# Closing LayerNorm of a two-layer trunk: a gate folded into the last weights, a square root by Sqrt and one Newton step, and two column parts centred on ScalarE and GpSimd

## Chip, cores and metric

One core of one Trainium2 chip runs the whole program. The metric is the device time of one execution, from the kernel's first to its last instruction with what lies around it. The kernel before took 1240.21 us (median of 3 runs, 1240.04 to 1242.66).

## What is computed

Two layers over 256 tokens of width 2048: a state-space mixer, then a dilated attention mixer whose keys and values come from the first layer's output. Each layer ends in the same way, and the change concerns the end of the second one:

```
def _layer_norm(x, g, b):
    xf = x.astype(jnp.float32)
    mu = jnp.mean(xf, -1, keepdims=True)
    var = jnp.mean(jnp.square(xf - mu), -1, keepdims=True)
    return ((xf - mu) * lax.rsqrt(var + LN_EPS)).astype(x.dtype) * g + b
...
    o = o.astype(h.dtype) * jax.nn.silu(z)
    return o @ out_w
...
        x = _layer_norm(DEEPNORM_ALPHA * x + (1.0 + gate) * y, ln_g[layer], ln_b[layer])
```

Here y is the mixer's product `o @ out_w`, gate a row of 2048 numbers (the kernel's copy of it has the 1 added already), g and b rows of 2048.

## The kernel before

Every product is made of float32 operands split in two halves that TensorE takes: a weight piece of 128x1024 is loaded into a tile `raw` (line 94, six buffers, issued by SyncE's queue), ScalarE copies it into `whi` (line 100), VectorE subtracts to get `wlo` (line 102), and three matmuls per pair of operands use them (lines 182 and 185 for the wide products, lines 213 to 215 for products with the tokens on the partitions). Four buffers each of `whi` and `wlo` let the two engines run ahead of TensorE.

The end of the program has these stages.

- `z_gate` (lines 1114 to 1122) makes the output gate of the attention heads. Beside it, jobs in the background call `hold` for six of the eight pieces of the last 1024 output columns' weights: loaded early, split early, kept in tiles that are free by then.
- The product `o @ out_w` follows. Columns 0 to 1023 go piece by piece for both halves of the tokens (called block 0 and block 1, the even and the odd tokens). For columns 1024 to 2047 all eight pieces are held, so that block 0 is finished first: `last(0, 0)`, `last(0, 1)`, then `last(1, 0)` and `last(1, 1)`, the last one as two halves of 256 columns.
- `join` (line 851 to 853, in `residual`) takes each product from PSUM: multiply by the gate (851), add alpha times the residual `u` (852), and gather statistics (853).
- `moments` (lines 855 to 866) turns the statistics into mean and 1/sqrt(variance). `rsqrt1` (lines 263 to 273) starts from a bit trick and takes three Newton steps, two VectorE instructions each (271, 272), on 128x1 tiles.
- Block 0 is then normalised by ScalarE (1193), multiplied by g on VectorE (`scaled`, line 1159) and added by four DMAs of GpSimd's queue (1213) to an output that holds b already.
- Block 1 comes last. TensorE centres three of its four column chunks: it copies u into PSUM by the identity (1206) and then adds a product of a diagonal matrix of minus the mean with the rows of g (1210), so that PSUM holds (u - mean) g. VectorE multiplies by 1/sqrt and adds b (1217, function `whole`). The fourth chunk goes through ScalarE (1214), `scaled` (1159) and an addition (1224). SyncE stores each chunk (1185).

Instructions of one engine run in the order in which they were recorded, with waits on semaphores for the others. The order is set by the recording layer's scheduler, and `tc.issue_after` pins some of it.

Of the kernel before, what the change touches and what calls it, by code (L numbers as in the profile page):

```python
# [18 lines left out]
P = 128  # L19
L = 256  # L20
D = 2048
# [7 lines left out]
ALPHA = 4.0 ** 0.25  # L29
EPS = 1e-5  # L30
# [19 lines left out]
def trunk(ctx, tc, xT, x, c, par, cst, bias, lnrow, ada, wdt, win, wxs, wout, wk, wv, wbin, wbout, out):  # L50
    nc = tc.nc
    V, S, T, PO = nc.vector, nc.scalar, nc.tensor, nc.gpsimd
# [28 lines left out]
    ident = cc[:, CI:CI + 128]  # L81
# [10 lines left out]
    def load_piece(src):  # L92
        raw = wp.tile([P, 1024], F32, name="raw", bufs=6)
        nc.sync.dma_start(raw, src)
        return raw

    def split(raw, into=None, after=None):

        hi, lo = into or [wp.tile([P, 1024], F32R, name=n, bufs=4) for n in ("whi", "wlo")]
        copied.append(S.activation(hi, raw, AF.Copy))  # L100
        with tc.issue_after(after) if after is not None else ExitStack():
            latest.append(V.tensor_tensor(lo, raw, hi.bitcast(F32), op=ALU.subtract))  # L102
        return hi.rearrange("p (k n) -> p k n", k=2), lo.rearrange("p (k n) -> p k n", k=2)
# [174 lines left out]
    gated = [dr.tile([D], F32, name=f"gated{i}", bufs=1) for i in range(2)]  # L278
# [56 lines left out]
    with ExitStack() as cA:  # L335
# [15 lines left out]
        with ExitStack() as cS:  # L351
# [78 lines left out]
            with ExitStack() as c0:  # L430
# [18 lines left out]
                first = [acc_pair(ex), acc_pair(ex)]  # L449
# [82 lines left out]
                begin, done, ended, halves = {}, set(), [], {}  # L532
# [127 lines left out]
            aux = cS.enter_context(tc.tile_pool(name="aux", bufs=2, space=PSUM, reuse_waits="tile"))  # L660
            aux2 = cS.enter_context(tc.tile_pool(name="aux2", bufs=2, space=PSUM, reuse_waits="tile"))
# [172 lines left out]
        aux = ctx.enter_context(tc.tile_pool(name="auxb", bufs=2, space=PSUM, reuse_waits="tile"))  # L834
# [11 lines left out]
        u = [pu.tile([P, D], F32, name=f"u{b}") for b in range(2)]  # L846
        st = [sm.tile([P, 5, 6], F32, name=f"st{b}", bufs=1) for b in range(2)]
# [7 lines left out]
        def moments(b, k, diag=None):  # L855

            mv = sm.tile([P, 2], F32, name=f"e{b}mv", bufs=1)
            V.bn_aggr(mv, st[b][:, 0:k, :])
            if diag is not None:
                V.tensor_scalar(diag, ident, mv[:, 0:1], -1.0, op0=ALU.mult, op1=ALU.mult)  # L860
            ve = sm.tile([P, 1], F32, name=f"e{b}ve", bufs=1)
            V.tensor_scalar(ve, mv[:, 1:2], EPS, 0.5, op0=ALU.add, op1=ALU.mult)
            r = rsqrt1(ve, f"e{b}")
            nb = sm.tile([P, 1], F32, name=f"e{b}nb", bufs=1)
            V.scalar_tensor_tensor(nb, mv[:, 0:1], -1.0, r, op0=ALU.mult, op1=ALU.mult)
            return r, nb
# [93 lines left out]
    with ExitStack() as cL:  # L960
# [15 lines left out]
        end, _ = x_quad(0)  # L976
# [55 lines left out]
    pc2 = cQ.enter_context(tc.tile_pool(name="pc2", bufs=2))  # L1032
# [92 lines left out]
    held = []  # L1125

    def hold(i, into=None):
        held.append(split(load_piece(wbout[2 + i // 4][i % 4]), into=into))

    def hold_in(i, k):  # L1130

        j = 4 + 2 * i + k
        if j < 12:
            return (slots if j < 8 else pb).tile([P, 1024], F32R, name=("s" if j < 8 else "b") + str(j))
        if i == 5:
            return pc2.tile([P, 1024], F32R, name="q2")
        return pc2.tile([P, 1024], F32R, name=("bs", "pT")[k], bufs=1)
# [3 lines left out]
    qs.append(queries(1))  # L1141
    attend(1, qs[1])
    state[0] = 0
    jobs.extend(lambda i=i: hold(i, [hold_in(i, k) for k in range(2)]) for i in range(6))
    for hq in range(2):
        z_gate(hq, qs[hq])
# [6 lines left out]
    def join(n, ps, b, i=None, c0=0, c1=512):  # L1153
        c = slice(512 * n + c0, 512 * n + c1)
        residual(n if i is None else i, ps, b, (gt[:, 0, c], gt[:, 1, c]), u[b][:, c], c)

    def scaled(b, c):

        V.tensor_tensor(u[b][:, c], u[b][:, c], lnt[:, 0, c], op=ALU.mult)
# [28 lines left out]
    for n in range(2):  # L1188
        last(0, n)
        join(2 + n, ps[n][0], 0)  # L1190
    r0, nb0 = moments(0, 4)
    for c in chunk:
        S.activation(u[0][:, c], u[0][:, c], AF.Identity, bias=nb0, scale=r0)
    last(1, 0)
    join(2, ps[0][1], 1)
    scaled(1, chunk[2])
# [6 lines left out]
    for c in chunk[:3]:  # L1203
        pt = (aux if len(cen) < 2 else aux2).tile([P, 512], F32, name="aux" if len(cen) < 2 else "po")
        with tc.issue_after(end.ins):
            T.matmul(pt, ident, u[1][:, c], start=True, stop=False)
        cen.append(pt)
    r1, nb1 = moments(1, 5, diag)
    for pt, c in zip(cen, chunk):
        T.matmul(pt, diag, lnt[:, 0, c], start=False, stop=True)  # L1210
    for c in chunk:
        scaled(0, c)
        nc.gpsimd.dma_start(rows(out, 0)[:, c], u[0][:, c], accum_op=ALU.add)
    S.activation(u[1][:, chunk[3]], u[1][:, chunk[3]], AF.Identity, bias=nb1, scale=r1)

    def whole(n):
        V.scalar_tensor_tensor(u[1][:, chunk[n]], cen[n], r1, lnt[:, 1, chunk[n]], op0=ALU.mult, op1=ALU.add)
        store(1, chunk[n])

    whole(0)  # L1220
    whole(1)
    scaled(1, chunk[3])
    whole(2)
    V.tensor_tensor(u[1][:, chunk[3]], u[1][:, chunk[3]], lnt[:, 1, chunk[3]], op=ALU.add)
    store(1, chunk[3])


def _cm(v):
# [88 lines left out]
```

## Time and profile before

| what | value |
|---|---|
| median of 3 runs | 1240.21 us (1240.04 to 1242.66) |
| the profiled execution | 1241.06 us |
| its span, first to last instruction | 1239.3 us |
| TensorE busy | 1227.7 us, 99% of the span |
| VectorE, ScalarE, GpSimd busy | 83%, 57%, 0% |
| granted TensorE clock | 0.998 |

Busy time says which engine worked, not what the end waited for. The chain of waits says that. Times inside the span count in microseconds from its start. A line of the timeline gives start, duration, engine, source line, operation and tiles, and in brackets how long the engine had been idle before it and what ended that.

### The profile page before, as it was taken

What the parts mean: (1) busy time and instruction counts of PE and PEld (TensorE: products, weight loads), DVE (VectorE), ACT (ScalarE), POOL (GpSimd) and SP (SyncE); (2) the same over time, 40 slices, a digit from 0 to 9 for tenths busy, and PEclk for the clock granted to TensorE, in tenths of its full rate; (3) what the DMA queues carried; (4) which work ended last, traced back from release to release, by engine and by line L of the source; (5) the groups of instructions that cost most, each with busy time, mean ns of one, the idle gap of its engine ahead of it and who ended that gap; (6) DMA issues with size and microseconds to landing.
All of it is one profiled execution on the core that took longest, in us unless ns stands there. A gap on an engine that the chain in (4) does not pass through costs nothing.

```text
span 1239.3 us, 18924 instructions
## 1 busy us (share of the span) xinstructions
PE 1227.7 (99%) x7178; PEld 1056.4 (85%) x7178; DVE 1026.7 (83%) x1454; ACT 702.1 (57%) x1048; POOL 3.8 (0%) x8
## 2 busy tenths in 40 slices
PE   9999999999999999999999999999999999999998
PEld 9889998898888888887888788888888888888886
DVE  6999986999987989899768678889978867658776
ACT  4555477868597789764335544434445645445631
POOL 0000000000000000000000000000000000000001
PEclk9999999999999999999999999999999999999999
DMA  9999977687656456699998569989997784464753
GB/s 368 422 421 422 421 256 248 231 288 257 215 192 210 164 172 202 215 338 338 365 317 294 193 201 354 372 340 369 381 384 293 231 260 136 134 203 121 226 217 68
DMA packets 81051, 335.90 MB, mean 271 GB/s; under 512 B 9168, under 2 KB 9408, under 8 KB 68160
## 3 DMA queue, kind: packets, MB, share of 16 engines
q1 hardware_dynamic: 80384, 333.65, 74.9%
q0 software_dynamic: 576, 1.05, 0.6%
q8 instruction: 56, 0.92, 0.3%
q14 instruction: 35, 0.29, 0.1%
HBM read 331.43 MB, written 3.23 MB: 270 GB/s over the span
## 4 chain that ended last, share of the span: by engine, by line
PE 89%; DMA 4%; DVE 4%; ACT 2%; issue 1%; DVEq 0%; SPq 0%; ACTq 0%
PE acc L182 24%; PE acc L214 12%; PE acc L215 12%; PE acc L213 12%; PE acc L185 12%; PE acc L151 3%; PE acc L153 3%; PE acc L152 3%; DMA raw<-in_win 2%; DMA araw<-in_ada 1%; PE py L758 1%; DVE wlo L102 1%; DVE araw L296 1%; ACT whi L100 1%; PE acc L968 1%
## 5 line engine op out<-in xcount | busy, mean ns | idle before, releaser
L100 ACT ACTIVATE whi<-raw 128x1024 fp32r<-128x1024 f32 x389 | 408.1, 1058 | 359.3 <-PE acc L215 140.7
L102 DVE TENSOR_TENSOR wlo<-raw,whi 128x1024 fp32r<-128x1024 f32 x389 | 469.4, 1223 | 141.5 <-ACT whi L100 137.4
L182 PE MATMUL acc<-actT,whi 128*128 128x512 f32 x1280 | 405.3, 397 | 0.0
L185 PEld LDWEIGHTS acc<-actT,wlo 128*128 128x128 f32 x1280 | 239.4, 188 | 55.6 <-DVE wlo L102 0.4
L214 PE MATMUL acc<-wlo,actT 128*128 128x512 f32 x656 | 257.1, 392 | 1.4 <-DVE wlo L102 1.4
L213 PE MATMUL acc<-whi,actT 128*128 128x512 f32 x656 | 253.6, 394 | 0.0
L185 PE MATMUL acc<-actT,wlo 128*128 128x256 f32 x1280 | 252.8, 279 | 0.0
L296 DVE SCALAR_TENSOR_TENSOR araw<-araw,cb__72 128x2048 f32<-128x2048 f32 x95 | 217.0, 2287 | 3.7 <-DMA araw<-in_ada 3.4
L182 PEld LDWEIGHTS acc<-actT,whi 128*128 128x128 f32 x1280 | 195.9, 189 | 0.4
L215 PE MATMUL acc<-whi,actT 128*128 128x512 f32 x432 | 168.9, 391 | 0.0
L214 PEld LDWEIGHTS acc<-wlo,actT 128*128 128x128 f32 x656 | 123.2, 188 | 27.6 <-DVE wlo L102 2.6
L213 PEld LDWEIGHTS acc<-whi,actT 128*128 128x128 f32 x656 | 122.8, 188 | 24.2
L151 PE MATMUL acc<-actT,whi 128*128 128x256 f32 x372 | 105.0, 285 | 0.9 <-ACT whi L100 0.9
L152 PE MATMUL acc<-actT,whi 128*128 128x256 f32 x372 | 104.4, 283 | 0.0
L153 PE MATMUL acc<-actT,wlo 128*128 128x256 f32 x372 | 102.5, 284 | 1.6 <-DVE wlo L102 1.6
L215 PEld LDWEIGHTS acc<-whi,actT 128*128 128x128 f32 x432 | 81.1, 188 | 16.7
L215 PE MATMUL acc<-whi,ylo 128*128 128x512 f32 x224 | 87.6, 391 | 0.0
L151 PEld LDWEIGHTS acc<-actT,whi 128*128 128x128 f32 x372 | 71.3, 192 | 1.9 <-ACT whi L100 1.3
L153 PEld LDWEIGHTS acc<-actT,wlo 128*128 128x128 f32 x372 | 70.0, 192 | 2.2 <-DVE wlo L102 2.0
L152 PEld LDWEIGHTS acc<-actT,whi 128*128 128x128 f32 x372 | 71.3, 192 | 0.3
L215 PEld LDWEIGHTS acc<-whi,ylo 128*128 128x128 f32 x224 | 42.1, 188 | 8.6
L716 ACT ACTIVATE seg<-cbc,cumT 128x128 f32<-128x128 f32 x128 | 41.0, 389 | 4.9 <-DVE wlo L102 2.3
(289 smaller groups left out, 1159.6 us busy)
## 6 DMA issues: line engine op xcount, KB each, us to landing
araw<-in_ada SPq DMA_DIRECT2D x96, 1024.0 KB, 7.3
raw<-in_win SPq DMA_DIRECT2D x109, 512.0 KB, 6.1
raw<-in_wout SPq DMA_DIRECT2D x64, 512.0 KB, 5.8
raw<-in_wbin SPq DMA_DIRECT2D x64, 512.0 KB, 3.8
raw<-in_wxs SPq DMA_DIRECT2D x48, 512.0 KB, 4.5
raw<-in_wv SPq DMA_DIRECT2D x48, 512.0 KB, 6.2
raw<-in_wk SPq DMA_DIRECT2D x48, 512.0 KB, 7.4
cbc<-cumd SPq DMA_DIRECT2D x16, 512.0 KB, 4.7
```

Source lines behind the costliest of these rows:

```text
L100: copied.append(S.activation(hi, raw, AF.Copy))
L102: latest.append(V.tensor_tensor(lo, raw, hi.bitcast(F32), op=ALU.subtract))
L151: T.matmul(o, hi[:, k, c_], ahi[:, kt, :], start=first, stop=False, skip_group_check=True)
L152: T.matmul(o, hi[:, k, c_], alo[:, kt, :], start=False, stop=False, skip_group_check=True)
L153: T.matmul(o, lo[:, k, c_], ahi[:, kt, :], start=False, stop=kt == k1 - 1, skip_group_check=True)
L182: T.matmul(ps[n], hi[:, k, n * P:n * P + P], both(kt), start=kt == 0, stop=False, skip_group_check=True)
L185: T.matmul(ps[n][:, 0, :], lo[:, k, n * P:n * P + P], high(kt), start=False, stop=kt == KT - 1, skip_group_check=True)
L213: T.matmul(o, h_, hi[:, k, :], start=kt == k0, stop=False, skip_group_check=part)
L214: T.matmul(o, h_, lo[:, k, :], start=False, stop=False, skip_group_check=part)
L215: end = T.matmul(o, l_, hi[:, k, :], start=False, stop=kt == k1 - 1, skip_group_check=part)
L296: return V.scalar_tensor_tensor(raw, raw, 1.0, cb_, op0=ALU.mult, op1=ALU.mult, accum_out=mod[layer][:, ct, j:j + 1])
L716: S.activation(seg[:, hh, b, :], cbc[:, hh, b, :], AF.Relu, bias=cumT[:, b, h0 + hh:h0 + hh + 1], scale=-1.0)
```

## The change

There are five parts.

1. The gate of columns 1792 to 2047 is loaded as `gcol` (256 columns, into the tile that the attention scores used, by SyncE's queue ahead of the held pieces) and multiplied into the weights of pieces 4 to 7 (new line 1131) before they are split. For those 256 columns the new function `weighed` (line 1196) reads the product from PSUM and adds alpha u in one instruction, where `join` needs two.
2. Block 0's statistics of the last 512 columns are taken as two parts of 256.
3. For block 1 the three Newton steps become ScalarE's Sqrt (1230), VectorE's reciprocal (1251) and one Newton step (1252, 1253). A Sqrt of a constant (1212) stands ahead of it, behind block 0's normalisation.
4. TensorE centres two chunks, not three. Of the others, columns 1024 to 1535 are centred by ScalarE (1236) and multiplied by g on GpSimd (1239); columns 1536 to 1791 are centred (1237) and multiplied (1239) on GpSimd; columns 1792 to 2047 are done by one VectorE instruction (1248).
5. All four chunks end in the same multiply-and-add by VectorE (1259) and a store. Two multiplications by g of block 1 (line 1159 before) are gone from VectorE.

```
 def hold(i, into=None):
-    held.append(split(load_piece(wbout[2 + i // 4][i % 4]), into=into))
+    raw = load_piece(wbout[2 + i // 4][i % 4])
+    if i >= 4:
+        part = raw.rearrange("p (k n) -> p k n", k=2)[:, :, 256:]
+        V.tensor_tensor(part, part, gcol[:, None, :].to_broadcast([P, 2, 256]), op=ALU.mult)
+    held.append(split(raw, into=into))
...
+gcol = pc2.tile([P, 512], F32, name="sc1", bufs=1)[:, :256]
+bcast(gcol, gated[1], D - 256)
...
+def weighed(b, part):
+    V.scalar_tensor_tensor(u[b][:, rest], u[b][:, rest], ALPHA, part, op0=ALU.mult, op1=ALU.add)
...
+with tc.issue_after(end.ins):
+    S.activation(sd, eps, AF.Sqrt)
...
-for h in range(2):
-    end = last(1, 1, slice(256 * h, 256 * h + 256), halves[h])
-    join(3, halves[h][1][:, 256 * h:256 * h + 256], 1, 3 + h, 256 * h, 256 * h + 256)
+end = last(1, 1, slice(0, 256), halves[0])
+join(3, halves[0][1][:, :256], 1, 3, 0, 256)
+end = last(1, 1, slice(256, 512), halves[1])
+weighed(1, halves[1][1][:, 256:])
+V.bn_stats(st[1][:, 4, :], u[1][:, rest])
...
-r1, nb1 = moments(1, 5, diag)
+V.bn_aggr(mv, st[1])
+S.activation(sd, mv[:, 1:2], AF.Sqrt, bias=eps)
+first = V.tensor_scalar(diag, ident, mv[:, 0:1], -1.0, op0=ALU.mult, op1=ALU.mult)
...
+S.activation(u[1][:, c2], u[1][:, c2], AF.Identity, bias=nm)
+nc.gpsimd.tensor_scalar(u[1][:, left], u[1][:, left], mv[:, 0:1], None, op0=ALU.subtract)
+for c in (left, c2):
+    nc.gpsimd.tensor_tensor(u[1][:, c], u[1][:, c], lnt[:, 0, c], op=ALU.mult)
...
+    first = V.scalar_tensor_tensor(u[1][:, rest], u[1][:, rest], mv[:, 0:1], lnt[:, 0, rest], op0=ALU.subtract,
+                                   op1=ALU.mult)
...
+    V.reciprocal(r1, sd)
+V.scalar_tensor_tensor(t1, r1, ve, r1, op0=ALU.mult, op1=ALU.mult)
+end = V.scalar_tensor_tensor(r1, t1, 1.5, r1, op0=ALU.add, op1=ALU.mult)
...
-whole(0)
-whole(1)
-scaled(1, chunk[3])
-whole(2)
-V.tensor_tensor(u[1][:, chunk[3]], u[1][:, chunk[3]], lnt[:, 1, chunk[3]], op=ALU.add)
-store(1, chunk[3])
+for n in range(4):
+    with tc.issue_after(end.ins):
+        end = V.scalar_tensor_tensor(u[1][:, chunk[n]], cen[n] if n < 2 else u[1][:, chunk[n]], r1,
+                                     lnt[:, 1, chunk[n]], op0=ALU.mult, op1=ALU.add)
+    store(1, chunk[n])
```

How the recorded order moves is shown at three places. The first is GpSimd's queue (POOL) at the end of the program; `u_5577` is block 0, `u_5578` block 1. Before, its last rows are:

```order
L1306 MEMSET const-uint8-127 128x1
L1313 UNCONDITIONAL_BRANCH [waits barrier_Pool_Activation_PE_DVE_SP_gather]
L1213 DMA out<-u_5577 128x512 [waits DMAHW3_49,DMAHW4_49,DMAHW2_49,DMAHW5_49,DMAHW1_49,DMAHW6_49,DMAHW0_49,DMAHW7_49,DVE_49,PE_49]
L1213 DMA out<-u_5577 128x512 [waits DVE_49] x3
L1313 UNCONDITIONAL_BRANCH
```

and with the change:

```order
L1256 DMA out<-u_5577 128x512 [waits DMAHW3_49,DMAHW4_49,DMAHW2_49,DMAHW5_49,DMAHW1_49,DMAHW6_49,DMAHW0_49,DMAHW7_49,DVE_49,PE_49]
L1256 DMA out<-u_5577 128x512 [waits DVE_49] x3
L1237 ISA
L1237 TENSOR_SCALAR u_5578<-u_5578,e1mv 128x256 [waits DVE_49,PE_49]
L1239 TENSOR_TENSOR u_5578<-u_5578,actT 128x512 [waits DMAHW2_49,Activation_49]
L1239 TENSOR_TENSOR u_5578<-u_5578,actT 128x256 [waits Pool_49]
L1349 UNCONDITIONAL_BRANCH
```

Behind the four DMAs now stand three instructions on tiles and, ahead of them, one without a tile (ISA). No line of the kernel asks for it: the build puts it ahead of the first TENSOR_SCALAR, and the built program names it PseudoReloadLibraryIndex, with index 0. The second place is VectorE (DVE) from block 1's statistics to the end; `sc` is the diagonal matrix, `e1y` the 1/sqrt, `aux` and `po` lie in PSUM. Before:

```order
L271 SCALAR_TENSOR_TENSOR e1t<-e1y,e1ve 128x1 [waits DVE_49]
L272 SCALAR_TENSOR_TENSOR e1y<-e1t,e1y 128x1 [waits DVE_49]
L865 SCALAR_TENSOR_TENSOR e1nb<-e1mv,e1y 128x1 [waits DVE_49]
L1217 SCALAR_TENSOR_TENSOR u_5578<-aux,e1y,actT 128x512 [waits DMAHW3_49,PE_49]
L1159 TENSOR_TENSOR u_5578<-u_5578,actT 128x512 [waits Activation_49]
L1217 SCALAR_TENSOR_TENSOR u_5578<-aux,e1y,actT 128x512 [waits PE_49]
L1217 SCALAR_TENSOR_TENSOR u_5578<-po,e1y,actT 128x512 [waits PE_49]
L1224 TENSOR_TENSOR u_5578<-u_5578,actT 128x512 [waits DVE_49]
```

and with the change:

```order
L1220 BN_STATS st_5580<-u_5578 128x6 [waits DVE_49]
L1229 BN_AGGR e1mv<-st_5580 128x2 [waits DVE_49]
L1231 TENSOR_SCALAR sc_11564<-cc,e1mv 128x128 [waits DVE_49]
L1234 TENSOR_SCALAR e1nb<-e1mv 128x1
L1246 TENSOR_SCALAR e1ve<-e1mv 128x1
L1248 SCALAR_TENSOR_TENSOR u_5578<-u_5578,e1mv,actT 128x256
L1251 RECIPROCAL e1y<-sd 128x1 [waits Activation_49]
L1252 SCALAR_TENSOR_TENSOR e1t<-e1y,e1ve 128x1 [waits DVE_49]
L1253 SCALAR_TENSOR_TENSOR e1y<-e1t,e1y 128x1 [waits DVE_49]
L1259 SCALAR_TENSOR_TENSOR u_5578<-aux,e1y,actT 128x512 [waits DMAHW4_49,DVE_49,PE_49]
L1259 SCALAR_TENSOR_TENSOR u_5578<-aux,e1y,actT 128x512 [waits PE_49]
L1259 SCALAR_TENSOR_TENSOR u_5578<-u_5578,e1y,actT 128x512 [waits Pool_49] x2
```

Eight small instructions between the statistics and the first store's instruction (one bit trick, six Newton halves, one for the mean) have become five and one of 256 columns, and the last two instructions before a store now wait for GpSimd. The third place is VectorE during `z_gate`, where `wlo`, `b`, `pT` and `q` are low halves of weights, `acc` is a product of TensorE, and `L1131` is the new multiplication by the gate:

```order
-L102 TENSOR_TENSOR b_11154<-raw,b_11153 128x1024
-L102 TENSOR_TENSOR wlo<-raw,whi 128x1024
+L102 TENSOR_TENSOR b_11156<-raw,b_11155 128x1024
 L243 TENSOR_TENSOR s_9373<-q_9376,s_9371 128x512
+L102 TENSOR_TENSOR wlo<-raw,whi 128x1024
+L1131 TENSOR_TENSOR raw<-raw,sc_10947 128x2x256 x2
+L102 TENSOR_TENSOR wlo<-raw,whi 128x1024
 L102 TENSOR_TENSOR pT<-raw,bs 128x1024
-L102 TENSOR_TENSOR q_11264<-raw,q_11263 128x1024
-L102 TENSOR_TENSOR wlo<-raw,whi 128x1024 x2
+L102 TENSOR_TENSOR q_11267<-raw,q_11266 128x1024
 L191 TENSOR_TENSOR q_9376<-acc,q_9376 128x256 x2
```

Two multiplications stand ahead of one `wlo`, and the next `wlo` has moved behind the two rows of line 191. The other two multiplications stand later, where `o @ out_w` begins.

More of the change, by code (lines that the diff above doesn't have):

```diff
@@ L1187, in trunk @@
     diag = pc2.tile([P, 512], F32, name="sc0", bufs=1)[:, :P]
[L1188 to L1191, printed above, removed]
[L1192 to L1193 removed]
+    def weighed(b, part):
+        V.scalar_tensor_tensor(u[b][:, rest], u[b][:, rest], ALPHA, part, op0=ALU.mult, op1=ALU.add)
+    rest = slice(D - 256, D)
+    last(0, 0)
+    join(2, ps[0][0], 0)
+    last(0, 1)
+    join(3, ps[1][0][:, :256], 0, 3, 0, 256)
+    weighed(0, ps[1][0][:, 256:])
+    V.bn_stats(st[0][:, 4, :], u[0][:, rest])
+    r0, nb0 = moments(0, 5)
+    for c in chunk:
+        end = S.activation(u[0][:, c], u[0][:, c], AF.Identity, bias=nb0, scale=r0)
+    eps = sm.tile([P, 1], F32, name="eps", bufs=1)
+    V.tensor_scalar(eps, ident[:, 0:1], 0.0, EPS, op0=ALU.mult, op1=ALU.add)
+    sd = sm.tile([P, 1], F32, name="sd", bufs=1)
+    with tc.issue_after(end.ins):
+        S.activation(sd, eps, AF.Sqrt)
     last(1, 0)
     join(2, ps[0][1], 1)
[L1196 removed]
     halves = [ps[1], [None, aux2.tile([P, 512], F32, name="po")]]
[L1198 to L1200 removed]
+    end = last(1, 1, slice(0, 256), halves[0])
[3 more added lines that the diff above has]
+    V.bn_stats(st[1][:, 4, :], u[1][:, rest])
     cen = []
[L1203 to L1204 removed]
+    for c in chunk[:2]:
+        pt = aux.tile([P, 512], F32, name="aux")
         with tc.issue_after(end.ins):
@@ L1207, in trunk @@
         cen.append(pt)
-    r1, nb1 = moments(1, 5, diag)
+    mv = sm.tile([P, 2], F32, name="e1mv", bufs=1)
+    V.bn_aggr(mv, st[1])
+    S.activation(sd, mv[:, 1:2], AF.Sqrt, bias=eps)
+    first = V.tensor_scalar(diag, ident, mv[:, 0:1], -1.0, op0=ALU.mult, op1=ALU.mult)
+    nm = sm.tile([P, 1], F32, name="e1nb", bufs=1)
+    with tc.issue_after(first.ins):
+        first = V.tensor_scalar(nm, mv[:, 0:1], -1.0, None, op0=ALU.mult)
+    left, c2 = slice(D - 512, D - 256), chunk[2]
+    S.activation(u[1][:, c2], u[1][:, c2], AF.Identity, bias=nm)
+    nc.gpsimd.tensor_scalar(u[1][:, left], u[1][:, left], mv[:, 0:1], None, op0=ALU.subtract)
+    for c in (left, c2):
+        nc.gpsimd.tensor_tensor(u[1][:, c], u[1][:, c], lnt[:, 0, c], op=ALU.mult)
     for pt, c in zip(cen, chunk):
         T.matmul(pt, diag, lnt[:, 0, c], start=False, stop=True)
+    ve = sm.tile([P, 1], F32, name="e1ve", bufs=1)
+    r1 = sm.tile([P, 1], F32, name="e1y", bufs=1)
+    t1 = sm.tile([P, 1], F32, name="e1t", bufs=1)
+    with tc.issue_after(first.ins):
+        first = V.tensor_scalar(ve, mv[:, 1:2], EPS, -0.5, op0=ALU.add, op1=ALU.mult)
+    with tc.issue_after(first.ins):
+        first = V.scalar_tensor_tensor(u[1][:, rest], u[1][:, rest], mv[:, 0:1], lnt[:, 0, rest], op0=ALU.subtract,
+                                       op1=ALU.mult)
+    with tc.issue_after(first.ins):
+        V.reciprocal(r1, sd)
+    V.scalar_tensor_tensor(t1, r1, ve, r1, op0=ALU.mult, op1=ALU.mult)
+    end = V.scalar_tensor_tensor(r1, t1, 1.5, r1, op0=ALU.add, op1=ALU.mult)
     for c in chunk:
```

3 lines of the change are left out of this document (removed).

## Prediction

> **What bounds the kernel now.** I read the busy table and the chain of waits first, for what the end waited on.
>
> ```profile
> PE 1227.7 (99%) x7178; PEld 1056.4 (85%) x7178; DVE 1026.7 (83%) x1454; ACT 702.1 (57%) x1048; POOL 3.8 (0%) x8
> ...
> PE 89%; DMA 4%; DVE 4%; ACT 2%; issue 1%; DVEq 0%; SPq 0%; ACTq 0%
> ```
>
> TensorE carries the program until the last product, so what is done beside it is free while it finds room. Only the stretch behind the last product is open. The timelines of TensorE (PE) and VectorE (DVE) there:
>
> ```profile
> 1228.28 0.28 PE L215 MATMUL po<-whi,s 128*128 128x256 f32 x1
> 1228.40 1.88 PE L1206 MATMUL aux<-u,cc 128*128 128x512 f32 x4
> 1230.12 1.02 PE L1206 MATMUL po<-u,cc 128*128 128x512 f32 x2
> 1230.98 1.88 PE L1210 MATMUL aux<-actT,sc 128*128 128x512 f32 x4
> ```
>
> ```profile
> 1226.28 0.41 DVE L851 TENSOR_TENSOR actT<-acc,actT 128x256 f32<-128x256 f32 x1
> 1226.60 0.68 DVE L1159 TENSOR_TENSOR u<-u,actT 128x512 f32<-128x512 f32 x1
> ...
> 1228.14 0.42 DVE L853 BATCH_NORM_STATS2 st<-u 128x6 f32<-128x256 f32 x1
> 1228.60 0.42 DVE L851 TENSOR_TENSOR actT<-po,actT 128x256 f32<-128x256 f32 x1
> 1229.06 0.42 DVE L852 SCALAR_TENSOR_TENSOR u<-u,actT 128x256 f32<-128x256 f32 x1
> 1229.52 0.43 DVE L853 BATCH_NORM_STATS2 st<-u 128x6 f32<-128x256 f32 x1
> 1229.98 0.29 DVE L858 BATCH_NORM_AGGREGATE e1mv<-st 128x2 f32<-128x30 f32 x1
> 1230.31 0.29 DVE L860 TENSOR_SCALAR sc<-cc,e1mv 128x128 f32<-128x128 f32 x1
> 1230.51 0.15 DVE L862 TENSOR_SCALAR e1ve<-e1mv 128x1 f32<-128x1 f32 x1
> ...
> 1231.78 0.22 DVE L271 SCALAR_TENSOR_TENSOR e1t<-e1y,e1ve 128x1 f32<-128x1 f32 x1
> 1232.04 0.16 DVE L272 SCALAR_TENSOR_TENSOR e1y<-e1t,e1y 128x1 f32<-128x1 f32 x1
> 1232.23 0.16 DVE L865 SCALAR_TENSOR_TENSOR e1nb<-e1mv,e1y 128x1 f32<-128x1 f32 x1
> 1232.32 0.75 DVE L1217 SCALAR_TENSOR_TENSOR u<-aux,e1y,actT 128x512 f32<-128x512 f32 x1
> ...
> 1234.54 0.74 DVE L1217 SCALAR_TENSOR_TENSOR u<-po,e1y,actT 128x512 f32<-128x512 f32 x1
> 1235.20 0.69 DVE L1224 TENSOR_TENSOR u<-u,actT 128x512 f32<-128x512 f32 x1
> ```
>
> The last product ends at 1228.28 + 0.28 = 1228.56 and VectorE takes it at 1228.60. It was busy until that moment too (1228.14 + 0.42). From there VectorE's work runs to 1235.20 + 0.69 = **1235.89**; the last store and the program's close follow (3.4 us of span), as they will after the change. I forecast the shift of 1235.89. The profiled execution took 1241.06 us, 0.85 over the median; a shift of it is added to the median, 1240.21.
>
> **The gate in the weights.** It adds four VectorE multiplications of 512 elements, 0.69 us each (the 128x512 row of line 851 below), beside `z_gate` and the product after it, and one more load ahead of a weight load on SyncE's queue.
>
> ```profile
> 1160.10 1.06 ACT L100 ACTIVATE q<-raw 128x1024 fp32r<-128x1024 f32 x1 [2.08 <-DMA raw<-in_wbout]
> ...
> 1162.34 2.35 DVE L102 TENSOR_TENSOR wlo<-raw,whi 128x1024 fp32r<-128x1024 f32 x2
> ...
> 1174.30 1.23 DVE L102 TENSOR_TENSOR wlo<-raw,whi 128x1024 fp32r<-128x1024 f32 x1 [1.56 <-ACT whi L100]
> ```
>
> The second multiplication needs the piece whose copy started at 1160.10 on its arrival; behind it the next `wlo` starts at about 1160.8, still before 1162.34, because two others moved behind it. Ten microseconds later VectorE waits for each copy (1.56 idle in the last row): the four buffers are full, and room is there. So I charge nothing; if TensorE were starved instead, the price is at most the two multiplications, 1.4 us (a rival below).
>
> **Before the last product.** Block 0's end, where VectorE had no room:
>
> ```profile
> 1217.41 0.69 DVE L851 TENSOR_TENSOR actT<-acc,actT 128x512 f32<-128x512 f32 x1 [3.29 <-PE acc L215]
> ...
> 1219.59 0.26 DVE L858 BATCH_NORM_AGGREGATE e0mv<-st 128x2 f32<-128x24 f32 x1
> ...
> 1222.66 0.69 DVE L1159 TENSOR_TENSOR u<-u,actT 128x512 f32<-128x512 f32 x1 [0.88 <-ACT u L1193]
> ```
>
> ```profile
> 1221.81 2.94 ACT L1193 ACTIVATE u<-u,e0nb,e0y 128x512 f32<-128x512 f32 x4 [19.66 <-DVE e0nb L865]
> ```
>
> ```profile
> 1152.94 1.28 ACT L1120 ACT_TABLE_LOAD   x1
> ```
>
> Three steps of 512 took 2.18 us here. Five of 256 on two independent halves take about 1.75: a 256-column step costs 0.32 when the next instruction doesn't need it (1226.28 to 1226.60) and 0.46 when it does. So, with 0.03 back for the wider aggregate, ScalarE starts 0.38 earlier, at 1221.43, and ends at 1224.37. VectorE's first multiplication for block 0 follows 0.85 behind that start, as in the last row: 1222.28. The second waits for ScalarE until 1222.99; five more instructions of 512 in steps of 0.60 put block 0's last one at 1225.39 and the next 256-column one at 1226.59, and with two steps of 0.46 VectorE is through near 1227.95: 0.65 us of slack, where there was none, since one multiplication of block 1 is gone from here. Sqrt's table load (1.28, the only such row nearby) ends at about 1225.7, four microseconds before the Sqrt that counts. It costs nothing while block 0's normalisation is done by 1228; uncovered it would cost 1.3.
>
> **Behind the last product.** One of three 256-column steps of 0.46 goes: the mean is there at 1229.85, not 1230.31. Diagonal matrix, negated mean, variance, the 256-column instruction (0.33 a step when independent), reciprocal, two halves of a Newton step follow:
>
> ```profile
> 1150.26 0.15 DVE L1095 RECIPROCAL den<-den 128x1 f32<-128x1 f32 x1
> 1150.33 0.40 DVE L191 TENSOR_TENSOR q<-acc,q 128x256 f32<-128x256 f32 x1
> ```
>
> The steps are 0.20 + 0.08 + 0.08 + 0.33 + 0.20 + 0.25 + 0.19 = 1.33 (0.08 as between the two rows here, 0.20 a dependent 128x1 of 0.16, 0.25 and 0.19 as between the rows from 1231.78), which gives 1231.18, against 1232.32 before. Sqrt's own 128x1 instruction on ScalarE has no row; it lies between 0.15 (VectorE's 128x1) and 0.81 (ScalarE's 128x512) and is wanted only at 1230.53, 0.7 after the mean: free up to there, 0.1 at the upper end. What is late next is TensorE: the diagonal matrix is ready at 1230.14 and its product starts at most 0.38 later (1230.60 to 1230.98 before), so the two chunks arrive at 1231.58 and 1232.44. With 0.66 for each of the other two, VectorE would end at 1234.45: **-1.44 us**, if GpSimd is in time.
>
> **GpSimd.** Its queue (POOL), its DMAs and its drain at the program's end:
>
> ```profile
> 1223.95 1.89 POOL L1213 DMA_DIRECT2D out<-u  x2 [1223.51 <-DVE actT L851]
> 1226.05 0.86 POOL L1213 DMA_DIRECT2D out<-u  x1 [0.20 <-issue]
> 1228.52 0.86 POOL L1213 DMA_DIRECT2D out<-u  x1 [1.61 <-DVE u L1159]
> ```
>
> ```profile
> L1313 POOLq DRAIN  x3: 34/108/5035, 1228.5 to 1239.0; - x3
> ```
>
> ```profile
> raw<-in_wk SPq DMA_DIRECT2D x48, 512.0 KB, 7.4
> ...
> actT<-in_lnrow SPq DMA_DIRECT2D x2, 1024.0 KB, 9.8
> ```
>
> The three new instructions stand behind those DMAs, and ahead of them the order shows one without a tile that reloads GpSimd's code. With block 0's first multiplication done at 1222.97 and its last at 1226.08, the DMAs' 0.6 lag and 0.9 each put the fourth at about 1226.7, and POOL is free at 1227.6; the reload cannot start before. No row shows a reload. From below its nearest row is ScalarE's table load, 1.28: then it ends before the mean is there and is free. From above it is the slowest landing in these rows, 9.8. A reload must fetch code from memory and stop the engine for it, so it is nearest to a load's landing; I take the slow common group, 7.4: POOL starts at 1235.0. Of the three instructions no row shows one on POOL either: VectorE's durations for these sizes sum to 0.42 + 0.69 + 0.42 = 1.53; at POOL's own 0.90 an instruction (mean of the four DMAs) they take 2.71, which I choose as rows of the same engine. The last product of POOL ends at 1237.71, and VectorE's last instruction, 0.05 + 0.69 later, at 1238.45: 1238.45 - 1235.89 = **+2.6 us**. The two centred chunks leave early and the other two late. POOL's ends shift this from -1.44 (load 1.28) through +1.4 (7.4 and 1.53) to +5.0 (9.8 and 2.71).
>
> The Trainium skill's page "GPSIMD Engine Reference", section "2.1 Instruction dispatch", says that the first call into freshly loaded GpSimd code pays some 6 us (5.95 measured) that no instruction in the profile shows. By that price the sum is an estimated +1.1 us; no run so far shows it.
>
> **Rivals.**
> - The reload is free or short (the code lies there already): -1.44, **1238.8**. For it: POOL has 2.2 us between its last DMA and the mean. Against it: nothing before has used such an instruction.
> - The reload waits until POOL's own transfers have landed. The drain row shows POOL standing 5.0 us behind the last one. Then it starts at 1226.7 + 5.04 = 1231.8, and the end is 4.2 later than forecast: +6.8, **1247.0**.
> - GpSimd is in time, but its 256-column product and VectorE's third last-stage instruction, which start together on the same tiles, follow one another instead: 0.66 less gain, -0.8, **1239.4**. The page "SBUF — State Buffer", section "Who interferes with whom", of the Trainium skill says so for a VectorE instruction with two SBUF inputs; no row here can show it.
> - TensorE starves at `z_gate` by the two multiplications: +1.4 on the first rival, **1240.2**.
>
> **How the numbers follow.** Forecast 0.55, short reload 0.17, drained reload 0.18, collision 0.06, starvation 0.04. The likeliest gives 1240.21 + 2.6 = **1242.8**, its own range 1238.8 to 1245.2. With the drained reload the range is 1238.4 to 1248.0; 0.2% (2.5 us) is about what a measurement can tell from none. A gain over 0.2% would need more than the 1.44 and all of GpSimd hidden: 0.03. The forecast lies on the edge, with 0.6 of it beyond; with the drained reload, slower has 0.51, within 0.2% has 0.46.
>
> **What would show it.** TensorE's last product at 1228.6 and VectorE idle just before it: the covered parts are right. Sqrt done before the reciprocal starts: right. VectorE idle before its last two instructions, released by POOL, and POOL's first product later than 1233: the reload. POOL's first product at 1230.2 instead would make the prediction wrong, and so would a wait of TensorE between 1155 and 1170.

## The result and the profile after

The changed kernel takes **1242.93 us** (median of 16 runs, 1242.46 to 1245.17), the kernel before 1240.24 beside it (16 runs, 1239.5 to 1242.8): a ratio of 1.0022, 95% interval 1.0014 to 1.003. The profiled execution took 1242.94 us with a span of 1241.2. That is 0.13 us from the forecast, by a sum whose largest term is not there. The times of one kernel often lie in two groups some 2 us apart (of the kernel before fourteen up to 1241.08 and two from 1242.66), so a median also depends on how many runs each group has, and one run of e12 below (1513.18 us at a granted clock of 0.751) is left out. The page of after, busy times and chain of waits:

```profile
PE 1230.0 (99%) x7174; PEld 1057.0 (85%) x7174; DVE 1028.1 (83%) x1455; ACT 704.2 (57%) x1051; POOL 6.8 (1%) x11
...
PE 93%; DVE 3%; DMA 2%; ACT 1%; issue 1%; DVEq 0%; ACTq 0%
```

TensorE is busy 2.3 us longer with four instructions fewer. Its timeline at the end:

```profile
1230.92 0.28 PE L215 MATMUL po<-whi,s 128*128 128x256 f32 x1
1231.04 1.88 PE L1226 MATMUL aux<-u,cc 128*128 128x512 f32 x4
1232.83 1.98 PE L1241 MATMUL aux<-actT,sc 128*128 128x512 f32 x4
```

The last product ends at 1231.20; before it was 1228.56. The whole slowdown, **+2.64 us, is there before the changed tail begins.** The tail itself is shorter. VectorE (DVE), ScalarE (ACT) and GpSimd (POOL) in after:

```profile
1231.24 0.42 DVE L1196 SCALAR_TENSOR_TENSOR u<-u,po 128x256 f32<-128x256 f32 x1 [0.53 <-PE po L215]
1231.70 0.43 DVE L1220 BATCH_NORM_STATS2 st<-u 128x6 f32<-128x256 f32 x1
1232.16 0.29 DVE L1229 BATCH_NORM_AGGREGATE e1mv<-st 128x2 f32<-128x30 f32 x1
1232.49 0.29 DVE L1231 TENSOR_SCALAR sc<-cc,e1mv 128x128 f32<-128x128 f32 x1
...
1232.81 0.57 DVE L1248 SCALAR_TENSOR_TENSOR u<-u,e1mv,actT 128x256 f32<-128x256 f32 x1
1233.31 0.15 DVE L1251 RECIPROCAL e1y<-sd 128x1 f32<-128x1 f32 x1
1233.50 0.22 DVE L1252 SCALAR_TENSOR_TENSOR e1t<-e1y,e1ve 128x1 f32<-128x1 f32 x1
1233.75 1.20 DVE L1253 SCALAR_TENSOR_TENSOR e1y<-e1t,e1y 128x1 f32<-128x1 f32 x1
1235.04 1.41 DVE L1259 SCALAR_TENSOR_TENSOR u<-aux,e1y,actT 128x512 f32<-128x512 f32 x2
1236.37 1.41 DVE L1259 SCALAR_TENSOR_TENSOR u<-u,e1y,actT 128x512 f32<-128x512 f32 x2
```

```profile
1227.15 1.28 ACT L1212 ACT_TABLE_LOAD   x1
...
1232.54 0.29 ACT L1230 ACTIVATE sd<-e1mv,eps 128x1 f32<-128x1 f32 x1 [3.89 <-DVE e1mv L1229]
1232.87 0.72 ACT L1236 ACTIVATE u<-u,e1nb 128x512 f32<-128x512 f32 x1
```

```profile
1226.34 3.72 POOL L1256 DMA_DIRECT2D out<-u  x4 [1225.91 <-DVE u L1165]
1232.64 0.93 POOL L1237 TENSOR_SCALAR u<-u,e1mv 128x256 f32<-128x256 f32 x1 [2.57 <-DVE e1mv L1229]
1233.67 1.95 POOL L1239 TENSOR_TENSOR u<-u,actT 128x512 f32<-128x512 f32 x2
```

From VectorE's first instruction on the last product to its last one it is 1231.24 to 1237.78, 6.54 us; before it was 7.29 (1228.60 to 1235.89). So the tail gained 0.75, and 2.64 - 0.75 = 1.89 is the difference of the spans (1241.2 - 1239.3). The rest up to the 2.69 between the medians is that the profiled execution of before lay 0.8 over its median.

Three things are to be seen. GpSimd starts 0.19 us after the mean is there (1232.45), so nothing of a reload is late. Line 1253, a 128x1 instruction of 0.16 us in the kernel before, takes 1.20, beside GpSimd's product from 1233.67. And VectorE waited 0.53 for TensorE at the first row: it was not what made TensorE late.

Where TensorE lost its time shows when the same stretch of the program is set side by side. The groups of TensorE's instructions that write `acc`, from 600 to 699 us, where nothing was changed (out<-streamed operand, operand held as weights; durations are minimum/median/maximum in ns), of before and of after:

```profile
L215 PE MATMUL acc<-whi,ylo x131: 389/389/392, 599.6 to 698.9; 128*128 128x512 f32 x131
L213 PE MATMUL acc<-whi,actT x130: 389/389/389, 599.9 to 698.5; 128*128 128x512 f32 x130
...
L213 PE MATMUL acc<-whi,xs x16: 389/389/389, 612.1 to 660.4; 128*128 128x512 f32 x16
```

```profile
L213 PE MATMUL acc<-whi,actT x127: 388/389/390, 599.8 to 698.4; 128*128 128x512 f32 x127
...
L215 PE MATMUL acc<-whi,ylo x127: 397/397/398, 600.3 to 698.8; 128*128 128x512 f32 x127
L213 PE MATMUL acc<-whi,xs x16: 393/396/399, 612.3 to 661.6; 128*128 128x512 f32 x16
```

Products with `actT` as weights are as fast as before; those with `ylo` or `xs` take 7 or 8 ns longer, with no wait before any of them. By the distance from one product's start to the next, over the whole trace, `ylo` goes from 228.8 to 236.3 ns (224 products, 1.68 us), `xs` from 231.3 to 236.8 (96, 0.52 us), and the products of `whi` and `wlo` with `s` into `acc` (12 of the 120 have 256 columns; one wait left out) from 218.0 to 222.3 (0.52 us): 2.7 us together, about the loss. After's first product with `ylo` starts 0.7 us earlier than before's (523.6 against 524.3), its last one 2.0 later (700.9 against 698.9): most of the loss is made in that stretch.

One wait comes beside it, which before doesn't have (engine and line, what it waited for, us in total, times, longest):

```profile
PE acc L215 <- DVE s L243: 0.3, 1, 0.3
```

It is at 1195.35. A multiplication by the gate (line 1131) had waited for its piece until 1191.13; line 243's instruction stood behind it on VectorE, and the product that needs it starts 0.74 us behind the one before it instead of 0.23. So in this execution a late piece, with the multiplication waiting for it, cost TensorE half a microsecond; what the multiplication itself adds to that wasn't separated. In e1 below, with the same instructions, the piece is there by 1187.50 and TensorE doesn't stand idle there.

What the three slower weights, `ylo`, `xs` and `s`, have in common is their place in memory. The change allocates two new small tiles, `eps` and `sd`, in a pool ahead of them; each holds 4 bytes per partition and takes up 32. Almost everything allocated behind moves by 64 bytes (`u` does not): `s0` from byte 122368 to 122432 of each partition, `xs`, `ylo` and the other large tiles after it likewise. `raw`, `whi`, `wlo` and `actT` lie ahead and stay. No instruction needs to differ for that, and the experiments start there.

### The profile page after: what moved, and what is told of

It reads as the page before. It is cut to its first block, busy times and chain, and to the rows that moved or that the text cites. A ratio compares the mean times of both kernels' runs of the same rounds, so it can differ in the third digit from the quotient of the medians.

```text
span 1241.2 us, 18930 instructions
## 1 busy us (share of the span) xinstructions
PE 1230.0 (99%) x7174; PEld 1057.0 (85%) x7174; DVE 1028.1 (83%) x1455; ACT 704.2 (57%) x1051; POOL 6.8 (1%) x11
## 4 chain that ended last, share of the span: by engine, by line
PE 93%; DVE 3%; DMA 2%; ACT 1%; issue 1%; DVEq 0%; ACTq 0%
PE acc L182 24%; PE acc L214 13%; PE acc L215 12%; PE acc L213 12%; PE acc L185 12%; PE acc L151 3%; PE acc L153 3%; PE acc L152 3%; PE py L758 1%; DVE wlo L102 1%; DMA araw<-in_ada 1%; PE acc L435 1%; DVE araw L296 1%; PE acc L968 1%; PE po L1099 1%; PE aux L811 1%
```

## The experiments

Theory: the 64 bytes cost TensorE its time. Rivals: the gate's multiplications or the new order delay it, or, as the prediction had it, GpSimd's reload costs the time.

**The displacement taken away from the changed kernel, and put into the kernel before.** The pool holds an unused spacer tile `pad` of 64 floats. e1_after_minus64 is the changed kernel with

```
-sm.tile([P, 64], F32, name="pad", bufs=1)
+sm.tile([P, 48], F32, name="pad", bufs=1)
```

> The changed kernel with its unused 256-byte spacer tile cut to 192 bytes, so that the 64 bytes that the two new small tiles take are given back and every large tile lies again where it lies in the kernel before; no instruction differs from the changed kernel. Theory (place in memory): the 2.64 us by which TensorE's last product came later are the price of the shift by 64 bytes; the product ends again near 1228.6 and the time is about 1239.5 (0.75 under the kernel before, the gain of the tail alone), at most 1240.0. Rival (instructions: the gate's multiplications, the early instruction for eps or the new order delay TensorE): the last product stays near 1231.2 and the time near 1242.9. Rival of the prediction (GpSimd's reload costs the time): no change by this edit, 1242.9.

e2_before_plus64 and e3_before_plus128 are the kernel before with 80 and 96 floats there:

> The kernel before with its spacer tile made 64 bytes longer: no instruction differs, and every tile behind it lies 64 bytes further, as in the changed kernel. Theory (place in memory): the last product comes about 2.6 us later, near 1231.2, and the time is about 1242.9. Rivals (the changed instructions, or GpSimd's reload): 1240.2, last product at 1228.6.

> The kernel before with its spacer tile made 128 bytes longer. If it is the start within 128 bytes that counts, all starts are multiples of 128 again and the time is 1240.2 with the last product at 1228.6. If any move of these tiles costs time (against the tiles that stay, say), it is near 1242.9. If both shifts leave 1240.2, the theory of the place in memory falls.

Measured, against 1240.65 for the kernel before beside them: e1 1239.67 (ratio 0.9993, 0.9984 to 1.0002), e2 1243.96 (1.0026, 1.0016 to 1.0036), e3 1243.96 (1.0027, 1.0018 to 1.0036). With the spacer cut the changed kernel loses its slowdown without any change of an instruction, and with a longer one the unchanged kernel has it: 3.3 us for either shift. VectorE takes the last product at 1227.97 in e1, at 1230.54 in e2 and at 1231.52 in e3 (1228.60 in before, 1231.24 in after). The rivals fall as causes of the slowdown. VectorE's tail in e1 is 6.52 us, as in after (6.54). A shift by 128 costs as much as one by 64, so a start at a multiple of 128 is not enough. The rows of e1, then of e2 and e3:

```profile
L215 PE MATMUL acc<-whi,ylo x130: 389/389/396, 600.1 to 698.7; 128*128 128x512 f32 x130
```

```profile
L215 PE MATMUL acc<-whi,ylo x127: 397/398/398, 599.9 to 698.4; 128*128 128x512 f32 x127
```

```profile
L215 PE MATMUL acc<-whi,ylo x127: 397/397/404, 600.2 to 698.7; 128*128 128x512 f32 x127
```

**Which displacement counts.** e5_before_plus256 has 128 floats in that spacer. e6_before_all_plus64 leaves it and lengthens another, ahead of `raw`, `whi`, `wlo` and `actT`; e12_weights_plus64 does both, with 112 floats in the second:

```
-cons.tile([P, 32], F32, name="pad")
+cons.tile([P, 48], F32, name="pad")
...
-sm.tile([P, 64], F32, name="pad", bufs=1)
+sm.tile([P, 112], F32, name="pad", bufs=1)
```

> The kernel before with its spacer tile made 256 bytes longer, all behind it 256 bytes further. Shifts by 64 and by 128 cost 3.3 us each. If the start within 256 bytes counts (all large tiles of the kernel before start at multiples of 256), the time is that of the kernel before, with its last product at the old place and 389 ns for the products with ylo as weights. If any displacement against the tiles that stay counts, or a start within 512 bytes, it is about 3.3 us slower and these products take 396 to 398 ns.

> The kernel before with another spacer, ahead of the buffers of weights and of actT, made 64 bytes longer: now the moving operands and actT lie 64 bytes further too, and the distances between the operands of the products named so far stay as they were. If the distance between a product's two operands counts, the time is that of the kernel before. If the start of the stationary operand itself counts, products with actT as weights become slower as well (389 to 396 or 398 ns a row), and as there are many times more of them the kernel is over 10 us slower.

> As the kernel before, with raw, whi, wlo and actT 64 bytes further and all tiles behind them 256 bytes further: the tiles that the change moved (s, xs, ylo and the rest) start at multiples of 256 again, while the operands streamed against them do not; their distance is 192 bytes over a multiple of 256. Theory (the distance between a product's two operands counts): the products with ylo, xs and s as weights take 395 to 398 ns again, those with actT 389, and these products alone cost about 2.6 us or more. Rival (the place of the weights' own tile counts): all 389. Beside it: if loads land at 12.3 us in the median of the stage from 20 to 165 us again (11.7 to 11.8 before), as in e6, raw or actT at 64 is enough for that and the place of araw is not needed; if at 11.7, as in e10, the place of araw and the tiles behind it is part of it.

The rows of e5, of e6 and of e12:

```profile
L215 PE MATMUL acc<-whi,ylo x130: 389/389/395, 600.1 to 698.7; 128*128 128x512 f32 x130
```

```profile
L215 PE MATMUL acc<-whi,ylo x130: 389/389/390, 599.8 to 698.4; 128*128 128x512 f32 x130
```

```profile
L215 PE MATMUL acc<-whi,ylo x128: 388/397/403, 599.7 to 698.8; 128*128 128x512 f32 x128
L213 PE MATMUL acc<-whi,actT x128: 387/389/398, 600.0 to 699.0; 128*128 128x512 f32 x128
...
L213 PE MATMUL acc<-whi,xs x16: 392/392/392, 615.2 to 664.3; 128*128 128x512 f32 x16
...
L215 PE MATMUL acc<-whi,xs x16: 388/388/389, 615.7 to 664.8; 128*128 128x512 f32 x16
```

A shift by 256 bytes costs nothing: 1240.36 against 1240.56 (ratio 1.0, 0.9991 to 1.0009). In e6 both operands of these products move by 64, and the products are fast again. In e12 the tiles held as weights start at multiples of 256 again and only the streamed operand is displaced: `ylo` is slow. So in the products of lines 213 to 215 it is **the distance between the streamed operand and the weights, modulo 256 bytes**, not the place of either: distances of 0 are fast, 64 and 128 are slow, and 192 is slow for `ylo`, while the rows of `xs` divide (392 for line 213, 388 for line 215). After shows it by itself too: from 1210 to 1228 us the products of `b` with `s`, both moved by 64, have 389 ns, those of `whi`, which stayed, with `s` 394. e12 takes 1243.92 against 1240.41 (1.0024, 1.0012 to 1.0035).

The distance isn't all, though. The wide products of line 182 are slow in the kernel before already, with both operands at multiples of 256:

```profile
L182 PE MATMUL acc<-actT,whi x13: 393/395/398, 1179.7 to 1183.9; 128*128 128x512 f32 x13
```

Over the whole trace their median is 396 in every run; why was not tested.

e6 is not free, though: 1242.59 (1.0016, 1.0008 to 1.0025), neither of what was expected. Its products are as fast as before; it waits for weights between 137 and 165 us. The loads of weights from 20 to 165 us, in before and in e6 (last column: median us from issue to landing):

```profile
raw<-in_win SPq DMA_DIRECT2D x50, 512.0 KB, 11.8
```

```profile
raw<-in_win SPq DMA_DIRECT2D x49, 512.0 KB, 12.3
```

e10_raw_plus64 asks whether the place of the loads' target does that:

```
-cons.tile([P, 32], F32, name="pad")
+cons.tile([P, 48], F32, name="pad")
...
+if not copied:
+    wp.tile([P, 48], F32, name="gap", bufs=1)
 halves[i] = [wp.tile([P, 1024], F32R, name=n, bufs=4) for n in ("whi", "wlo")]
```

> As the kernel before, but the buffers into which the weights are loaded (raw) start 64 bytes further, and whi, wlo, actT and all behind them 256 bytes further: only raw leaves its place within 256 bytes (with the small constants ahead of it). In e6, where all of these moved by 64, the products were as fast as before, while loads landed 0.8 us later and TensorE waited for weights between 137 and 165 us. Theory (the place that a transfer writes to costs the 2.0 us there): the same again, 2.0 over the kernel before, loads at 12.5 instead of 11.7. Rival (something else in e6, such as the place of whi or actT in itself): the time of the kernel before.

It took 1241.03 against 1240.28 (1.0006, 0.9997 to 1.0015), not 2.0 more. That theory falls: `raw` at 64 is not enough for e6's loss, and neither are `raw`, `whi` and `actT` together in e12, which lies 3.5 over the kernel before, hardly more than e2 and e3 (3.3). The landing alone says little: it is 11.7 in e10 and e12, but 12.0 and 12.1 in e2 and e3, where `raw` stays. The rate tells more: from 100 to 137 us the loads run at 414 GB/s in e6, at 421 in e10 and e12, at 423 in before. That TensorE doesn't wait in the traces of e10 and e12 shows less, since it started later there (98 products by 20 us, 116 in before). What slows the loads of e6 stays open.

**The Newton step.** In e1 as in after the second Newton instruction takes 1.20 us. e4_newton_scalars is e1 with

```
-V.scalar_tensor_tensor(t1, r1, ve, r1, op0=ALU.mult, op1=ALU.mult)
-end = V.scalar_tensor_tensor(r1, t1, 1.5, r1, op0=ALU.add, op1=ALU.mult)
+V.tensor_scalar(t1, r1, ve, r1, op0=ALU.mult, op1=ALU.mult)
+end = V.tensor_scalar(r1, t1, 1.5, r1, op0=ALU.add, op1=ALU.mult)
```

> As e1_after_minus64, and the Newton step's two VectorE instructions take the variance and the root as scalars per partition instead of as a second tensor, with the same result. Theory (a VectorE instruction with two tensors from SBUF waits for a GpSimd instruction of the same kind): the second of them, 1.20 us in the changed kernel and 0.16 elsewhere, falls to about 0.2; the four last VectorE instructions start 1.0 earlier and the time is about 1238.5 (at most 1.0 under e1), less if GpSimd's two products, which end near the third of them, are late next. Rival (it waits for something else, such as its operand): the instruction stays near 1.2 and the time equals e1.

GpSimd's first product in e1, 512 columns, starts at 1230.40. Its group (busy us, mean ns, idle before it):

```profile
L1239 POOL TENSOR_TENSOR u<-u,actT 128x512 f32<-128x512 f32 x1 | 1.3, 1262 | 0.1
```

So it ends at 1231.66. VectorE in e1, and then in e4:

```profile
1230.22 0.22 DVE L1252 SCALAR_TENSOR_TENSOR e1t<-e1y,e1ve 128x1 f32<-128x1 f32 x1
1230.47 1.20 DVE L1253 SCALAR_TENSOR_TENSOR e1y<-e1t,e1y 128x1 f32<-128x1 f32 x1
1231.76 1.41 DVE L1259 SCALAR_TENSOR_TENSOR u<-aux,e1y,actT 128x512 f32<-128x512 f32 x2
```

```profile
1228.22 0.42 DVE L1196 SCALAR_TENSOR_TENSOR u<-u,po 128x256 f32<-128x256 f32 x1 [0.67 <-PE po L215]
...
1230.48 0.27 DVE L1252 TENSOR_SCALAR e1t<-e1y,e1ve 128x1 f32<-128x1 f32 x1
1230.79 0.21 DVE L1253 TENSOR_SCALAR e1y<-e1t,e1y 128x1 f32<-128x1 f32 x1
1231.10 1.48 DVE L1259 SCALAR_TENSOR_TENSOR u<-aux,e1y,actT 128x512 f32<-128x512 f32 x2
1232.50 1.41 DVE L1259 SCALAR_TENSOR_TENSOR u<-u,e1y,actT 128x512 f32<-128x512 f32 x2
```

In e1 the instruction ends at 1231.67, with GpSimd's. Written with scalars it takes 0.21, while GpSimd's product (1230.65 in e4) runs beside it as before. The tail is 5.69 us, and the kernel takes **1238.52** (0.9982, 0.9973 to 0.9991): less than the kernel before and than e1 (1239.67).

e9_pool_one_tensor turns it round: Newton's instructions as in e1, and GpSimd's with one tensor, which leaves out the multiplication by g.

```
-nc.gpsimd.tensor_tensor(u[1][:, c], u[1][:, c], lnt[:, 0, c], op=ALU.mult)
+nc.gpsimd.tensor_scalar(u[1][:, c], u[1][:, c], 1.0, None, op0=ALU.mult)
```

> As e1_after_minus64 (Newton step in its first form, with a second tensor), but GpSimd's two products take one tensor and a constant: the multiplication by the norm's weight in block 1's columns 1024 to 1535 and 1536 to 1791 is left out. Theory (the Newton step waited because both engines ran an instruction with two tensors from SBUF): its second instruction falls from 1.20 to about 0.2 and VectorE's end comes 1.0 earlier behind the last product (5.5 instead of 6.5). Rival (any GpSimd instruction on SBUF holds it up, or its operand is late): it stays near 1.2.

```profile
1231.64 0.55 DVE L1253 SCALAR_TENSOR_TENSOR e1y<-e1t,e1y 128x1 f32<-128x1 f32 x1
```

0.55: less than 1.20, but not the 0.2 expected; the tail is 5.89, not 5.5 (1238.88, 0.9986, 0.9976 to 0.9995). So beside a GpSimd instruction with one tensor VectorE's two-tensor instruction is longer as well (0.16 in the kernel before), but ends long before GpSimd's, which takes 1.49.

**The reload.** e7_free_pool is e4 with a GpSimd instruction that waits for nothing, behind the four DMAs (and 8 floats less in the spacer):

```
+free = sm.tile([P, 1], F32, name="free", bufs=1)
+with tc.issue_after(dma.ins):
+    nc.gpsimd.tensor_scalar(free, ident[:, 0:1], 0.0, EPS, op0=ALU.mult, op1=ALU.add)
```

> As e4_newton_scalars, with one more GpSimd instruction of 128x1, which needs nothing and whose result nobody uses, right behind block 0's four transfers; the spacer gives back its 32 bytes. It shows the reload by itself, which the wait for the mean covers otherwise. The reload took at most 2.69 us there (the idle row of GpSimd's first instruction in e4). Theory (reload short and covered): the free instruction starts between 0.1 and 2.7 us behind the last transfer and the time stays at 1238.5. The prediction's forecast (7.4 us) and the page's 6 us would put it at least 6 us behind; then the three products would be late, which they are not in the changed kernel.

The rows that stand on GpSimd's sequencer (POOLq) in e7 where the recorded order has the reload, and GpSimd's timeline:

```profile
L1259 POOLq MODIFY_POOL_CONFIG  x2: 421/421/421, 1225.9 to 1226.0; - x2
```

```profile
1222.58 3.73 POOL L1256 DMA_DIRECT2D out<-u  x4 [1222.15 <-DVE u L1165]
1226.04 0.59 POOL L1259 TENSOR_SCALAR free<-cc 128x1 f32<-128x1 f32 x1
```

The two rows take 0.42 us each, side by side, and the instruction behind them starts at most 0.2 us after the first of them, while the last DMA is still shown. The time is 1238.49 (0.9984, 0.9975 to 0.9994). The reload costs nothing that the trace can show.

**The gate and the centring.** e8_no_gate_in_weights is e4 with `join` for the last 256 columns again:

```
-if i >= 4:
-    part = raw.rearrange("p (k n) -> p k n", k=2)[:, :, 256:]
-    V.tensor_tensor(part, part, gcol[:, None, :].to_broadcast([P, 2, 256]), op=ALU.mult)
...
-weighed(1, halves[1][1][:, 256:])
-V.bn_stats(st[1][:, 4, :], u[1][:, rest])
+join(3, halves[1][1][:, 256:], 1, 4, 256, 512)
```

> As e4_newton_scalars, but the gate is multiplied into the product again as in the kernel before (three VectorE instructions for each block's last 256 columns), not into the weights; all tiles lie as before. Theory (the gate costs TensorE nothing and takes one dependent 256-column step out of the tail): VectorE has the mean 0.46 us later behind the last product, that product itself does not move, and the time is 0.46 over e4, about 1239.0. Rival (the gate's multiplications or the wait for its column block delay TensorE by up to 1.4 us): the last product comes earlier here by as much, and the time is e4's or below.

VectorE in e8, from the last product to the mean:

```profile
1229.15 0.42 DVE L851 TENSOR_TENSOR actT<-po,actT 128x256 f32<-128x256 f32 x1 [0.56 <-PE po L215]
1229.61 0.42 DVE L852 SCALAR_TENSOR_TENSOR u<-u,actT 128x256 f32<-128x256 f32 x1
1230.07 0.43 DVE L853 BATCH_NORM_STATS2 st<-u 128x6 f32<-128x256 f32 x1
1230.53 0.29 DVE L1222 BATCH_NORM_AGGREGATE e1mv<-st 128x2 f32<-128x30 f32 x1
```

The aggregate comes 1.38 us behind the first row, in e4 0.92 (1228.22 to 1229.14): the step is 0.46, as expected. The time is 1240.41 (0.9996, 0.9987 to 1.0005), 1.9 over e4, more than expected, and the last product comes 0.93 later than in e4, not earlier. Most of that isn't the edit's. 0.7 of the 0.93 is there at 699 us already, where the two kernels don't differ (the last product with `ylo` starts at 698.9 in e4 and at 699.6 in e8). And the medians mix unlike groups: nine of e4's eleven times lie from 1237.85 to 1239.05, but only five of e8's from 1238.78 to 1239.55, the other six from 1240.41 up. The medians of the lower groups, 1238.46 and 1238.84, differ by 0.38, near the step. Where the other 0.2 us by which the last product is later come from wasn't separated. The rival, that the gate delays TensorE, has the wrong sign here; the half microsecond in after's trace came with a late piece.

e11_scalar_centres is e4 with both parts centred by ScalarE:

```
-S.activation(u[1][:, c2], u[1][:, c2], AF.Identity, bias=nm)
-nc.gpsimd.tensor_scalar(u[1][:, left], u[1][:, left], mv[:, 0:1], None, op0=ALU.subtract)
+for c in (left, c2):
+    S.activation(u[1][:, c], u[1][:, c], AF.Identity, bias=nm)
```

> As e4_newton_scalars, but ScalarE centres both parts (256 columns, then 512), and GpSimd only multiplies. It asks whether GpSimd's centring instruction, with one tensor, holds up VectorE's 256-column instruction beside it (0.57 us there, 0.42 elsewhere). If it does: 0.42, the reciprocal and all behind it 0.15 earlier, 1238.4. If GpSimd's product, which now starts earlier, holds it up instead: up to 0.7 later, 1239.2. If neither: the time of e4.

```profile
1229.34 0.47 DVE L1248 SCALAR_TENSOR_TENSOR u<-u,e1mv,actT 128x256 f32<-128x256 f32 x1
...
1230.55 1.58 DVE L1259 SCALAR_TENSOR_TENSOR u<-aux,e1y,actT 128x512 f32<-128x512 f32 x2
```

Without GpSimd's centring beside it line 1248 takes 0.47 instead of 0.57; the first two final instructions then take 1.58 instead of 1.48, and the tail is 5.67, that of e4 (5.69). The time is 1238.91 (0.9994, 0.9985 to 1.0003), not separable from e4.

## Why the prediction was right in time and wrong in cause

- **That nothing is lost before the last product** failed, and this is the step that decides. The sum had TensorE's last product at 1228.6; it came at 1231.20. The working covered every instruction that was added and moved, and left out what two allocations do to the addresses of everything behind them. The runs put 3.3 us on that (e2, e3), and taking it away gives 1239.67 (e1).
- **The reload of 7.4 us** failed. It was sized by the landing of a weight load; the trace shows 0.4 us, and no delay of the next instruction (e7). The sign named for it, a first product of GpSimd later than 1233, did appear (1233.67), but only because everything behind the last product lies 2.64 later: GpSimd started 0.19 after the mean, and VectorE never waited for it ahead of its last two instructions. The rival "The reload is free or short" holds, and the drained reload falls. The Trainium skill, in "GPSIMD Engine Reference", section "2.1 Instruction dispatch", has some 6 us for the first call into freshly loaded code; e7 shows at most 0.2.
- **The collision** was a rival of 0.06 with a gain of 0.8. It is what happened: 0.75 in after, 0.77 in e1. The place was another: not VectorE's third final instruction but the 128x1 Newton instruction, which ran into GpSimd's product. The page "SBUF — State Buffer" of the Trainium skill, section "Who interferes with whom", states that a VectorE instruction with two SBUF inputs and a GpSimd instruction that reads SBUF exclude one another. The ends at 1231.67 and 1231.66 in e1 agree with it, and so does e4, where one input and scalars take 0.21. Beside GpSimd instructions with one tensor the traces differ from it: in e9 the wait is only part of GpSimd's 1.49 us, and line 1248, with two inputs from SBUF, runs within GpSimd's centring (1232.64 to 1233.57 in after) and takes 0.57, against 0.47 in e11 without it.
- **-1.44 with GpSimd in time** was right: e4, without that collision, has a tail of 5.69 against 7.29, -1.60.
- **GpSimd's three instructions** were taken at 2.71; they take 0.93 + 1.95 = 2.88. **The table load is covered**: right (1227.15 to 1228.43; Sqrt done at 1232.83, the reciprocal at 1233.31). **The slack of VectorE before the last product** was 0.65; the trace has 0.53, and 0.67 in e4. **The gate** takes 0.46 out of the tail: right (e8). That it costs TensorE nothing holds in e1 and e4; in after TensorE lost half a microsecond behind a multiplication that waited for its piece, at 1195, not between 1155 and 1170, where the prediction looked for a wait.

So +2.6 for the reload was 0, and +2.6 for the addresses was not in the sum. That both are nearly the same is chance.

## What to carry to other kernels

When a tile is added to a pool, look at what moves behind it: here two tiles of four bytes moved the rest by 64, which cost 3.3 us (e2), more than the change could gain, and a spacer that restored the old distances (or rounding the addition up to 256 bytes, by e5) takes it back. When a kernel slows where nothing was edited, compare the same product's row in both traces before looking at the edit. Beside GpSimd's work, write VectorE's small instructions with scalars per partition instead of a second tensor.

## What the runs showed of the hardware

- In the products of lines 213 to 215 a float32 matmul of 512 columns has 389 ns in the trace when streamed operand and weights lie a multiple of 256 bytes apart, and with `ylo` 397 at distances of 64, 128 and, in e12, 192 bytes. The loads of weights keep their 187 to 188 ns. Line 182's products have 393 to 398 at a distance of 0 too, so this is no rule for every product. The Trainium skill's page "TensorE: Matmul & The Clock Gate", section "Step-by-step: what each phase is for", says that TensorE reads both through ports of their own and that loading the next weights takes nothing from the running product; here the products depend on the two places together. That loading and streaming meet in memory is an inference; the runs show only the dependence on the distance.
- A 128x1 VectorE instruction with two tensors took 1.20 us beside GpSimd's 512-column product and 0.55 beside one with a single tensor, instead of 0.16; with scalars 0.21.
- With all large buffers moved by 64 bytes (e6) the loads of weights ran at 414 GB/s from 100 to 137 us instead of 423, and at 421 when only some of them were (e10, e12); not explained.
